# mLSTM outputs: the weights' upper part meets both parts of the values at once, and the sums lie in a pair of PSUM banks

## The chip, the cores and the metric

The kernel runs on one core of a Trainium2 chip. The metric is the device time of one execution in microseconds; shorter is better. The core's engines are TensorE (PE in the profile, with PEld for its weight loads), VectorE (DVE), ScalarE (ACT), GpSimd (POOL) and SyncE (SP, which issues most DMAs).

## The reference

One encoder layer over a prompt of 1024 tokens and a sample of 2048 tokens, each with 16 learned meta tokens in front. One input projection feeds two branches: neighbourhood attention and a bidirectional mLSTM. Both are gated, projected, merged and sent through an output projection. What matters here is the mLSTM output of one chunk (4 heads of 128; each direction has its own gates):

```python
S = jnp.einsum('bhnjd,bhnsd->bhnjs', q, k) * jnp.exp(logD - m_t[..., None])
e_inter = jnp.exp(inter - m_t)
num = jnp.einsum('bhnjs,bhnsv->bhnjv', S, v) + e_inter[..., None] * jnp.einsum('bhnvk,bhnjk->bhnjv', Cs, q)
den = jnp.sum(S, axis=-1) + e_inter * jnp.einsum('bhnk,bhnjk->bhnj', ns, q)
h = num / jnp.maximum(jnp.abs(den), jnp.exp(-m_t))[..., None]
```

Inputs and outputs are float32.

## The kernel before

**Products in two parts.** A float32 operand is split into an upper part (rounded to the type that PE multiplies in one pass, `F32R`) and a lower part (the rest). `mm3` makes one product out of three PE matmuls: upper by upper, upper by lower, lower by upper (lines 172, 173, 174). The same lines appear in the profile for every user of `mm3`, so tiles tell the users apart.

**Two streams of work in one order.** `dense` (input projection, merge, output projection) and `sparse` (mLSTM and attention of both sequences) are Python generators. `run` takes a step of the sparse one and then steps of the dense one in proportion to a rate, so PE's instructions are interleaved in an order fixed by hand. PE runs that order as it stands. The order on the other engines is planned by a scheduler that simulates the program; semaphores are put in by the framework. A tile with `bufs=n` rotates through n buffers, and the writer of a buffer waits for all readers of the tile that had it before.

**The mLSTM stage** (`ml`, once per sequence) first runs a gate chain (`ml_gates`, small matmuls, transposes and scans for both directions in turn), then for each of 4 heads `ml_states` (backward over blocks of 256 tokens, two chunks of 128 each) and `ml_outputs` (forward over blocks: 4 in the prompt, 8 in the sample, so 48 blocks and 96 chunks in all). In `ml_outputs`, for a block: `scores` multiplies keys by queries into bank `sc`; `weigh` applies decay and splits the result into `sh` and `sl`; `values` splits the values; `back(b, j)` for each of the two chunks j multiplies the query by the state (`pi`, 260 columns, in a `tr` bank), lets ACT scale that into `num` (line 1829), then multiplies the weights by the values, for each direction d with one `mm3` of 130 columns (128 values, a column of ones, one of zeros), and lets DVE add this to `num` (line 1834). `finish` divides. `back(p, 0)` and `back(p, 1)` of a block lie two steps of the generator apart, with dense work and `weigh`, `split`, `mask`, `chain` of the next block between.

**PSUM.** There are 8 banks of 512 floats per partition: tag `pj` has 3, `tr` 2, `sc` 1, `sm` 2. In the mLSTM stage `sm` serves the gate chain (one bank per small step), `pd` in `ml_states` (one bank per chunk), and `pa` in `back` (one bank per chunk, both directions side by side). In the attention stage `sm` serves scores and outputs.

```python
BANKS = dict(pj=3, tr=2, sc=1, sm=2)
```

Of the kernel before, what the change touches and what calls it, by code (L numbers as in the profile page):

```python
# [10 lines left out]
F32 = mybir.dt.float32  # L11
F32R = mybir.dt.float32r
I32 = mybir.dt.int32
AF = mybir.ActivationFunctionType
ALU = mybir.AluOpType
PSUM = bass.MemoryType.PSUM
DRAM = bass.MemoryType.DRAM

P = 128
# [18 lines left out]
CB = 2  # L38
# [88 lines left out]
class K:  # L127
# [36 lines left out]
            self.tc.keep_in_program_order(x)  # L164

    def psum(self, tag, shape):
        return self.pp.tile(shape, F32, name=tag, tag=tag, bufs=BANKS[tag])

    def mm3(self, out, ah, al, bh, bl, start=True, stop=True, **more):

# [6 lines left out]
    def setup(self, ctx):  # L177
        tc, nc, i = self.tc, self.nc, self.i
        self.cp = cp = ctx.enter_context(tc.tile_pool(name="cp", bufs=1))
        self.dp = dp = ctx.enter_context(tc.tile_pool(name="dp", bufs=1, space=DRAM))  # L180
        self.pp = ctx.enter_context(tc.tile_pool(name="pp", bufs=2, space=PSUM))
        self.ident = cp.tile([P, P], F32, name="ident")
        nc.sync.dma_start(self.ident, i["eye"])
        warm = cp.tile([P, 1], F32, name="warm")
        nc.gpsimd.memset(warm, 0.0)
        nc.scalar.activation(warm, warm, AF.Square)
        self.ones = cp.tile([P, P], F32, name="ones")
        nc.gpsimd.memset(self.ones, 1.0)
        p = self.psum("sm", [P, 4, P])
        o = self.ones.rearrange("p (a b) -> p a b", a=1).to_broadcast([P, 4, P])  # L190
        for _ in range(4):
            nc.tensor.matmul(p, self.ones, o, start=True, stop=True)
# [1235 lines left out]
    def ml_gates(self, s, keep, mp, res):  # L1428
# [33 lines left out]

        def one(d):
            l2 = lf[:, d].rearrange("p c h -> p (c h)")
            pb = self.psum("sm", [P, 512])
            nc.tensor.matmul(pb[:, :NR], self.tri[:, d, :], l2, start=True, stop=True)
            bT = t(f"g_b{d}", [P, NC_, 4])
            nc.vector.tensor_copy(bT.rearrange("p c h -> p (c h)"), pb[:, :NR])
            aT = kt(f"g_a{d}")
            nc.vector.tensor_tensor(aT, gv[:, d, 0], bT, op=ALU.subtract)  # L1470
            aTf = aT.rearrange("p c h -> p (c h)")
            yield
            pa = self.psum("sm", [P, 512])
            nc.tensor.transpose(pa[:NR, :P], aTf, self.ident)
            aR = t("g_aR", [NR, P], bufs=2)
            nc.scalar.activation(aR, pa[:NR, :P], AF.Copy)
            yield
            cm = t("g_cm", [NR, P], bufs=2)
            rv = (lambda x: x) if d == 0 else (lambda x: x[:, ::-1])
            nc.vector.tensor_tensor_scan(out=rv(cm), data0=rv(aR), data1=rv(aR), initial=-3.0e38, op0=ALU.max, op1=ALU.max)  # L1480
            end = P - 1 if d == 0 else 0
            pg = self.psum("sm", [P, 512])
            nc.tensor.matmul(pg[0:1, :NR], self.ones[:, 0:1], l2, start=True, stop=True)
            rg = t("g_rg", [1, NR], bufs=2)
            nc.scalar.activation(rg, pg[0:1, :NR], AF.Copy)
            yield
            px = self.psum("sm", [P, 512])
            nc.tensor.transpose(px[0:1, :NR], cm[:, end:end + 1], self.ident[:NR, :NR])
            ra = t("g_ra", [1, NR], bufs=2)
            nc.vector.tensor_tensor(ra, px[0:1, :NR], rg, op=ALU.add)  # L1490
            me = t("g_me", [1, NR], bufs=2)
            mpv = t("g_mp", [1, NR], bufs=2)
            nc.gpsimd.memset(mpv, 0.0)
            yield
            for h in range(4):
                w = slice(h, NR, 4)
                nc.vector.tensor_tensor_scan(out=rv(me[:, w]), data0=rv(rg[:, w]), data1=rv(ra[:, w]), initial=0.0,
                                             op0=ALU.add, op1=ALU.max)
            if d == 0:
                nc.vector.tensor_copy(mpv[:, 4:], me[:, :NR - 4])  # L1500
            else:
                nc.vector.tensor_copy(mpv[:, :NR - 4], me[:, 4:])
            yield
            pm = self.psum("sm", [P, 512])
            nc.tensor.transpose(pm[:NR, 0:1], mpv, self.ident[0:1, 0:1])
            mpc = t("g_mpc", [NR, 1], bufs=2)
            nc.vector.tensor_copy(mpc, pm[:NR, 0:1])
            uR = t("g_uR", [NR, P], bufs=2)
            nc.vector.tensor_scalar(uR, cm, mpc, -1.0, op0=ALU.max, op1=ALU.mult)
            nc.sync.dma_start(self.UD[s].rearrange("h c d t -> c h d t")[:, :, d, :], uR)  # L1510
            uend = t("g_ue", [NR, 1], bufs=2)
            nc.vector.tensor_copy(uend, uR[:, end:end + 1])
            nc.scalar.activation(cm, uR, AF.Exp, bias=mpc)
            nc.scalar.activation(aR, aR, AF.Exp, bias=uend)
            fs = t("g_fs", [NR, 1], bufs=2)
            nc.scalar.activation(fs, uend, AF.Exp, bias=mpc)
            yield
            pu = self.psum("sm", [P, 512])
            nc.tensor.transpose(pu[:, :NR], uR, self.ident[:NR, :NR])
            em = kt(f"g_em{d}")  # L1520
            nc.vector.tensor_tensor(em.rearrange("p c h -> p (c h)"), pu[:, :NR], bT.rearrange("p c h -> p (c h)"), op=ALU.subtract)
            nc.scalar.activation(em, em, AF.Exp)
            dg = t("g_dg", [NR, NR], bufs=2)
            nc.vector.tensor_scalar(dg, self.ident[:NR, :NR], fs, None, op0=ALU.mult)
            yield
            for name, x in (("e", cm), ("w", aR)):
                pe = self.psum("sm", [P, 512])
                nc.tensor.transpose(pe[:, :NR], x, self.ident[:NR, :NR])
                eT = kt(f"g_{name}T{d}")
                nc.vector.tensor_copy(eT.rearrange("p c h -> p (c h)"), pe[:, :NR])  # L1530
                out[d][name] = eT
                yield
            pf = self.psum("sm", [P, 512])
            nc.tensor.matmul(pf[:, :NR], self.ones[:NR, :], dg, start=True, stop=True)
            fsb = kt(f"g_fb{d}")
            nc.vector.tensor_copy(fsb.rearrange("p c h -> p (c h)"), pf[:, :NR])
            out[d].update(a=aT, em=em, f=fsb)
# [59 lines left out]
    def ml(self, s):  # L1597
# [3 lines left out]
        with tc.tile_pool(name=f"mg{s}", bufs=1, side="right", reuse_waits="tile") as keep:  # L1601
            with tc.tile_pool(name=f"mt{s}", bufs=1, side="right", reuse_waits="tile") as mp:
# [4 lines left out]
                    nc.sync.dma_start(self.trim[:, j], self.i["trimask"])  # L1607
                g = []
                yield from self.ml_gates(s, keep, mp, g)
            with tc.tile_pool(name=f"ml{s}", bufs=1, side="right", reuse_waits="tile") as mp:  # L1610
                self.vas = [mp.tile([P, CB, 130], F32, name=f"va{j}") for j in range(3)]
                for va in self.vas:
                    nc.gpsimd.memset(va[:, :, 128:129], 1.0)
# [17 lines left out]
                while norms:  # L1631
# [2 lines left out]
                    n += 1  # L1634
                    yield A_A
        self.done.add(("ml", s))

    def vload(self, mp, s, h, tok, np_, nch):
        nc = self.nc
# [6 lines left out]
    def ml_states(self, mp, s, h, g, NB, sts):  # L1646
# [34 lines left out]
        for i in range(N):  # L1681
# [13 lines left out]
            yield A_D  # L1695
            vwh, vwl = vws.pop(i)
            if not c0:
                pd = self.psum("sm", [P, 512])
                self.mm3(pd[:, :130], kth[:NM, 0, :], ktl[:NM, 0, :], vwh[:NM, 0, 0, :], vwl[:NM, 0, 0, :])
                nc.scalar.activation(sts[0][:, 0, 0:130], pd[:, :130], AF.Copy)  # L1700
                yield A_D
                continue
# [3 lines left out]
                nc.gpsimd.memset(sts[b][:, CB - 1, 130:260], 0.0)  # L1706
            if b:
                sts[b - 1] = mp.tile([P, CB, 260], F32, name="st", bufs=NB)
            for j in range(CB - 1, -1, -1):
                cc = b * CB + j  # L1710
                pd = self.psum("sm", [P, 512])
                self.mm3(pd[:, :260], kth[:, j, :], ktl[:, j, :],
                         vwh[:, j].rearrange("p d c -> p (d c)"), vwl[:, j].rearrange("p d c -> p (d c)"))
                if cc + 1 < NB * CB:
# [6 lines left out]
    def ml_outputs(self, mp, s, h, g, NB, sts, norms):  # L1721
# [44 lines left out]
        def values(b):  # L1766

            if b < NB:
                va = vas.pop(b)
                vh = mp.tile([P, CB, 130], F32R, name="vh", bufs=1)  # L1770
                vl = mp.tile([P, CB, 130], F32R, name="vl", bufs=1)
                nc.scalar.activation(f2(vh), f2(va), AF.Copy)
                nc.vector.tensor_tensor(f2(vl), f2(va), f2(vh).bitcast(F32), op=ALU.subtract)
                vs[b] = vh, vl

        def chain(b):

# [39 lines left out]

        def back(b, j):
            sh, sl = shs[b]
            (vh, vl), qx = vs[b], qks[b][:, 0]  # L1820
            cch, ccl = cs[b]
            cc = 1 + b * CB + j
            pi = self.psum("tr", [P, 512])
# [3 lines left out]
            num = nums[b]  # L1827
            for d in range(2):
                nc.scalar.activation(num[:, j, d], pi[:, 130 * d:130 * d + 130], AF.Copy, scale=g[d]["e"][:, cc, h:h + 1])
            pa = self.psum("sm", [P, 512])  # L1830
            for d in range(2):
                self.mm3(pa[:, 130 * d:130 * d + 130], sh[:, j, d, :], sl[:, j, d, :], vh[:, j, :], vl[:, j, :])
            nj = num[:, j].rearrange("p d c -> p (d c)")
            nc.vector.tensor_tensor(nj, pa[:, :260], nj, op=ALU.add)

        def finish(b):
            num = nums.pop(b)
# [429 lines left out]
```

## Time and profile before

| what | value |
|---|---|
| median of 3 runs (lowest, highest) | 2720.48 us (2719.08, 2722.17) |
| profiled execution, its time | 2718.74 us |
| its span in the profile | 2717.0 us |
| PE busy | 2686.7 us, 99% |
| DVE busy | 1766.1 us, 65% |
| ACT busy | 1520.2 us, 56% |
| granted PE clock, mean | 0.998 |

A row of a group reads: line, engine, operation, output<-inputs by tile names, partitions x elements, count, then time. A row of the timeline reads: start in us from the span's start, duration in us, engine, line, operation, tiles, shapes, count, and in brackets the idle time of the engine before it with what ended that. Durations on PE overlap, since matmuls are pipelined; the distance from one start to the next tells what one costs. A row of a stretch of time gives, after the stretch, the busy time of PE, PEld, DVE, ACT and POOL (with counts), the granted clock, the DMA share and the bandwidth. A row of waits reads: who waited on whose tile, then microseconds in total, times, longest.

### The profile page before, as it was taken

Reading aid. Unit: us, or ns where it says so; the run is one execution under the profiler, and the core shown is the slowest. Engines: PE = TensorE matmul, PEld = TensorE weight load, DVE = VectorE, ACT = ScalarE, POOL = GpSimd, SP = SyncE. Lnnn points to the kernel's source line nnn. Section 1 sums busy time; section 2 is a strip of 40 time slices with the busy share of each in tenths; the row PEclk is TensorE's granted clock in tenths of the full one; section 3 lists DMA queues with packets and bytes.
Section 4 is the critical chain, followed back from the end, with each engine's and each line's share of the span. In section 5 each row is a group of like instructions: output and inputs, shape, how many; then the busy total and the mean of one; then the engine's idle time right before and its main releaser. Section 6 shows DMA issues by size and latency. Waiting matters only on the chain.

```text
span 2717.0 us, 47583 instructions
## 1 busy us (share of the span) xinstructions
PE 2686.7 (99%) x16696; PEld 2394.5 (88%) x16696; DVE 1766.1 (65%) x4376; ACT 1520.2 (56%) x3375; POOL 126.0 (5%) x294
## 2 busy tenths in 40 slices
PE   9999999999999999999999999999999999999998
PEld 7999988879998889998878888888879898989988
DVE  5557765535777747775424857574658879687864
ACT  5233354435555656666535757564648686767641
POOL 0005000005000013000000000000000000000000
PEclk9999999999999999999999999999999999999999
DMA  9984454369865797757486666786599999898955
GB/s 369 340 283 143 138 187 158 102 239 343 265 222 174 264 325 227 229 175 234 144 294 191 222 202 209 262 278 201 163 299 332 313 298 295 245 317 244 324 208 220
DMA packets 351507, 657.53 MB, mean 242 GB/s; under 512 B 53444, under 2 KB 158868, under 8 KB 351268
## 3 DMA queue, kind: packets, MB, share of 16 engines
q1 hardware_dynamic: 344004, 645.46, 71.7%
q0 software_dynamic: 7264, 9.04, 1.2%
q8 instruction: 131, 2.15, 0.3%
q14 instruction: 108, 0.88, 0.1%
HBM read 438.64 MB, written 215.66 MB: 241 GB/s over the span
## 4 chain that ended last, share of the span: by engine, by line
PE 88%; DMA 7%; DVE 2%; ACT 2%; issue 1%; SPq 1%; POOL 0%; DVEq 0%; ACTq 0%; POOLq 0%
PE pj L172 14%; PE pj L173 14%; PE pj L174 14%; PE pj L644 5%; PE pj L645 5%; PE pj L646 5%; PE sm L1407 3%; PE pj L2042 2%; PE pj L2044 2%; PE pj L2043 2%; PE tr L1393 2%; PE sm L174 2%; PE sm L173 2%; PE sm L172 2%; DMA wraw<-wu 1%; DMA wlo<-wl 1%
## 5 line engine op out<-in xcount | busy, mean ns | idle before, releaser
L172 PE MATMUL pj<-xh,whi 128*128 128x512 f32 (+1 forms) x1480 | 580.2, 392 | 4.6 <-ACT st L569 3.6
L173 PE MATMUL pj<-xl,whi 128*128 128x512 f32 (+1 forms) x1480 | 565.8, 382 | 0.2 <-DVE xl L345 0.2
L174 PE MATMUL pj<-xh,wlo 128*128 128x512 f32 (+1 forms) x1480 | 565.1, 382 | 0.3 <-DVE wlo L272 0.3
L644 PE MATMUL pj<-whi,xh 128*128 128x256 f32 (+1 forms) x1152 | 330.9, 287 | 0.0
L174 PEld LDWEIGHTS pj<-xh,wlo 128*128 128x128 f32 x1480 | 278.2, 188 | 58.2 <-DVE wlo L272 0.6
L172 PEld LDWEIGHTS pj<-xh,whi 128*128 128x128 f32 x1480 | 278.5, 188 | 54.1 <-ACT st L569 4.4
L645 PE MATMUL pj<-wlo,xh 128*128 128x256 f32 (+1 forms) x1152 | 325.0, 282 | 0.6 <-DMA wlo<-wl 0.6
L646 PE MATMUL pj<-whi,xl 128*128 128x256 f32 (+1 forms) x1152 | 324.8, 282 | 0.0
L173 PEld LDWEIGHTS pj<-xl,whi 128*128 128x128 f32 x1480 | 278.8, 188 | 46.2 <-issue 0.7
L2042 PE MATMUL pj<-whi,mh 128*128 128x256 f32 x768 | 220.3, 287 | 0.0
L645 PEld LDWEIGHTS pj<-wlo,xh 128*128 128x128 f32 x1152 | 217.1, 188 | 0.9 <-DMA wlo<-wl 0.8
L644 PEld LDWEIGHTS pj<-whi,xh 128*128 128x128 f32 x1152 | 217.3, 189 | 0.4
L646 PEld LDWEIGHTS pj<-whi,xl 128*128 128x128 f32 x1152 | 217.0, 188 | 0.0
L2043 PE MATMUL pj<-wlo,mh 128*128 128x256 f32 x768 | 217.0, 283 | 0.0
L2044 PE MATMUL pj<-whi,mlo 128*128 128x256 f32 x768 | 216.9, 282 | 0.0
L1396 DVE TENSOR_TENSOR pts<-tr,pts 96x384 fp32r<-96x384 f32 (+2 forms) x192 | 118.5, 617 | 64.7 <-ACT pts L1395 63.8
L172 PE MATMUL pj<-yh,whi 128*128 128x512 f32 x384 | 154.2, 401 | 1.8 <-DVE tg L2009 1.1
L173 PE MATMUL pj<-yl,whi 128*128 128x512 f32 x384 | 151.0, 393 | 0.2 <-DVE yl L1420 0.2
L174 PE MATMUL pj<-yh,wlo 128*128 128x512 f32 x384 | 151.0, 393 | 0.0
L2043 PEld LDWEIGHTS pj<-wlo,mh 128*128 128x128 f32 x768 | 146.1, 190 | 1.0
L2042 PEld LDWEIGHTS pj<-whi,mh 128*128 128x128 f32 x768 | 146.0, 190 | 1.0
L2044 PEld LDWEIGHTS pj<-whi,mlo 128*128 128x128 f32 x768 | 145.9, 190 | 0.0
(459 smaller groups left out, 6171.7 us busy)
## 6 DMA issues: line engine op xcount, KB each, us to landing
whi<-wh SPq DMA_DIRECT2D x140, 512.0 KB
wlo<-wl SPq DMA_DIRECT2D x140, 512.0 KB
wraw<-wu SPq DMA_DIRECT2D x64, 512.0 KB
wh<-whi SPq DMA_DIRECT2D x64, 512.0 KB
wl<-wlo SPq DMA_DIRECT2D x64, 512.0 KB
gt<-st SPq DMA_DIRECT2D x96, 256.0 KB
tg<-gt SPq DMA_DIRECT2D x96, 256.0 KB
xt<-xt SPq DMA_DIRECT2D x32, 512.0 KB
```

Of the source, the lines that this page charges most:

```text
L172: mm(out, ah, bh, start=start, stop=False, **more)
L173: mm(out, ah, bl, start=False, stop=False, **more)
L174: mm(out, al, bh, start=False, stop=stop, **more)
L644: nc.tensor.matmul(o, xh, wh, start=k == 0, stop=False)
L645: nc.tensor.matmul(o, xh, wl, start=False, stop=False)
L646: nc.tensor.matmul(o, xl, wh, start=False, stop=k == KT - 1)
L1393: nc.tensor.transpose(pt[:ks, ch, :], pr_[:, ch * ks:(ch + 1) * ks], self.ident)
L1396: nc.vector.tensor_tensor(pts[:ks, :nb, 1, :], pt[:ks, :nb], pts[:ks, :nb, 0, :].bitcast(F32), op=ALU.subtract)
L1407: nc.tensor.matmul(av[:, cb % 2], vt[:ks, kc // 8 + ch].rearrange("p a b -> p (a b)"), pts[:ks, ch].rearrange("p a b -> p (a b)"), start=c ...
L2042: nc.tensor.matmul(o, mh[:, f, xs], q, start=fresh and f == 0, stop=False, skip_group_check=True)
L2043: nc.tensor.matmul(o, mh[:, f, xs], w[1][:, k, :], start=False, stop=False, skip_group_check=True)
L2044: nc.tensor.matmul(o, ml[:, f, xs], q, start=False, stop=f == KT - 1, skip_group_check=True)
```

## The change

- `values` writes both parts into one tile `v` of shape [P, 2, 2, 130], part by part next to each other within a chunk.
- `back` takes a pair of banks for a chunk, one bank for a direction. For each direction the lower part of the weights meets the upper part of the values (130 columns), then the upper part of the weights meets both parts in one matmul of 258 columns: columns 0 to 129 accumulate, columns 130 to 257 are a sum of their own. DVE adds the first 130 columns of both banks to `num`, and then the other 128 columns of both.
- The two banks of `sm` get a pool of their own that is closed in the mLSTM's states and outputs. There a pool `pl` holds one tile of two banks: `pa` of `back`, and in `ml_states` one tile for both chunks of a block.
- The gate chain takes its banks from `tr` instead of `sm`.
- In `setup` the tags `pj`, `tr` and `sc` are allocated once at the start.

```diff
     def psum(self, tag, shape):
-        return self.pp.tile(shape, F32, name=tag, tag=tag, bufs=BANKS[tag])
+        return (self.pm if tag == "sm" else self.pp).tile(shape, F32, name=tag, tag=tag, bufs=BANKS[tag])
+
+    def small(self, on):
+
+        if on:
+            self.sms = ExitStack()
+            self.pm = self.sms.enter_context(self.tc.tile_pool(name=f"pm{len(self.done)}", bufs=2, space=PSUM))
+        else:
+            self.sms.close()
...
         self.pp = ctx.enter_context(tc.tile_pool(name="pp", bufs=2, space=PSUM))
+        for tag in ("pj", "tr", "sc"):
+            self.psum(tag, [P, 512])
+        self.small(True)
+        ctx.callback(lambda: self.small(False))
...
         def one(d):
             l2 = lf[:, d].rearrange("p c h -> p (c h)")
-            pb = self.psum("sm", [P, 512])
+            pb = self.psum("tr", [P, 512])
...
                 yield from self.ml_gates(s, keep, mp, g)
-            with tc.tile_pool(name=f"ml{s}", bufs=1, side="right", reuse_waits="tile") as mp:
+            self.small(False)
+            with tc.tile_pool(name=f"ml{s}", bufs=1, side="right", reuse_waits="tile") as mp, \
+                 tc.tile_pool(name=f"pl{s}", bufs=1, space=PSUM) as self.pl:
...
         self.done.add(("ml", s))
+        self.small(True)
...
             if not c0:
-                pd = self.psum("sm", [P, 512])
+                pd = self.pl.tile([P, 2, 512], F32, name="pa")[:, 0]
...
+            pds = self.pl.tile([P, CB, 512], F32, name="pa")
             for j in range(CB - 1, -1, -1):
                 cc = b * CB + j
-                pd = self.psum("sm", [P, 512])
+                pd = pds[:, j]
...
-                vh = mp.tile([P, CB, 130], F32R, name="vh", bufs=1)
-                vl = mp.tile([P, CB, 130], F32R, name="vl", bufs=1)
-                nc.scalar.activation(f2(vh), f2(va), AF.Copy)
-                nc.vector.tensor_tensor(f2(vl), f2(va), f2(vh).bitcast(F32), op=ALU.subtract)
-                vs[b] = vh, vl
+                v = vs[b] = mp.tile([P, CB, 2, 130], F32R, name="vh", bufs=1)
+                nc.scalar.activation(v[:, :, 0], va, AF.Copy)
+                nc.vector.tensor_tensor(v[:, :, 1], va, v[:, :, 0].bitcast(F32), op=ALU.subtract)
...
-            pa = self.psum("sm", [P, 512])
+            pa = self.pl.tile([P, 2, 512], F32, name="pa")
             for d in range(2):
-                self.mm3(pa[:, 130 * d:130 * d + 130], sh[:, j, d, :], sl[:, j, d, :], vh[:, j, :], vl[:, j, :])
-            nj = num[:, j].rearrange("p d c -> p (d c)")
-            nc.vector.tensor_tensor(nj, pa[:, :260], nj, op=ALU.add)
+                nc.tensor.matmul(pa[:, d, 0:130], sl[:, j, d, :], v[:, j, 0], start=True, stop=False, skip_group_check=True)
+                nc.tensor.matmul(pa[:, d, 0:258], sh[:, j, d, :], v[:, j].rearrange("p a c -> p (a c)")[:, 0:258], start=False, stop=True, skip_group_check=True)
+            nj = num[:, j]
+            nc.vector.tensor_tensor(nj, pa[:, :, 0:130], nj, op=ALU.add)
+            nc.vector.tensor_tensor(nj[:, :, 0:P], pa[:, :, 130:258], nj[:, :, 0:P], op=ALU.add)
```

The seven other places of the gate chain change from `sm` to `tr` in the same way.

More of the change, by code (lines that the diff above doesn't have):

```diff
@@ L1472, in one @@
             yield
-            pa = self.psum("sm", [P, 512])
+            pa = self.psum("tr", [P, 512])
             nc.tensor.transpose(pa[:NR, :P], aTf, self.ident)
@@ L1481, in one @@
             end = P - 1 if d == 0 else 0
-            pg = self.psum("sm", [P, 512])
+            pg = self.psum("tr", [P, 512])
             nc.tensor.matmul(pg[0:1, :NR], self.ones[:, 0:1], l2, start=True, stop=True)
@@ L1486, in one @@
             yield
-            px = self.psum("sm", [P, 512])
+            px = self.psum("tr", [P, 512])
             nc.tensor.transpose(px[0:1, :NR], cm[:, end:end + 1], self.ident[:NR, :NR])
@@ L1503, in one @@
             yield
-            pm = self.psum("sm", [P, 512])
+            pm = self.psum("tr", [P, 512])
             nc.tensor.transpose(pm[:NR, 0:1], mpv, self.ident[0:1, 0:1])
@@ L1517, in one @@
             yield
-            pu = self.psum("sm", [P, 512])
+            pu = self.psum("tr", [P, 512])
             nc.tensor.transpose(pu[:, :NR], uR, self.ident[:NR, :NR])
@@ L1526, in one @@
             for name, x in (("e", cm), ("w", aR)):
-                pe = self.psum("sm", [P, 512])
+                pe = self.psum("tr", [P, 512])
                 nc.tensor.transpose(pe[:, :NR], x, self.ident[:NR, :NR])
@@ L1532, in one @@
                 yield
-            pf = self.psum("sm", [P, 512])
+            pf = self.psum("tr", [P, 512])
             nc.tensor.matmul(pf[:, :NR], self.ones[:NR, :], dg, start=True, stop=True)
@@ L1819, in back @@
             sh, sl = shs[b]
-            (vh, vl), qx = vs[b], qks[b][:, 0]
+            v, qx = vs[b], qks[b][:, 0]
             cch, ccl = cs[b]
@@ L1829, in back @@
                 nc.scalar.activation(num[:, j, d], pi[:, 130 * d:130 * d + 130], AF.Copy, scale=g[d]["e"][:, cc, h:h + 1])
-            pa = self.psum("sm", [P, 512])
+            pa = self.pl.tile([P, 2, 512], F32, name="pa")
             for d in range(2):
-                self.mm3(pa[:, 130 * d:130 * d + 130], sh[:, j, d, :], sl[:, j, d, :], vh[:, j, :], vl[:, j, :])
-            nj = num[:, j].rearrange("p d c -> p (d c)")
-            nc.vector.tensor_tensor(nj, pa[:, :260], nj, op=ALU.add)
+                nc.tensor.matmul(pa[:, d, 0:130], sl[:, j, d, :], v[:, j, 0], start=True, stop=False, skip_group_check=True)
[3 more added lines that the diff above has]
+            nc.vector.tensor_tensor(nj[:, :, 0:P], pa[:, :, 130:258], nj[:, :, 0:P], op=ALU.add)
         def finish(b):
```

## Prediction

> **What bounds the kernel now.** I read the page first: the span and the busy line.
>
> ```profile
> span 2717.0 us, 47583 instructions
> ...
> PE 2686.7 (99%) x16696; PEld 2394.5 (88%) x16696; DVE 1766.1 (65%) x4376; ACT 1520.2 (56%) x3375; POOL 126.0 (5%) x294
> ```
>
> PE is idle for 30 us of 2717 and runs one order written out by hand, so the time is the sum of what its instructions take plus what it waits. Anything that shortens PE work shortens the span, as long as no other engine makes PE wait. VectorE (DVE) has room on average, but the average hides the mLSTM stages, so next I looked up the changed instructions by tile (count, shortest/median/longest in ns, first and last start, shapes).
>
> ```profile
> L1834 DVE TENSOR_TENSOR num<-sm,num x96: 393/428/430, 665.8 to 1977.8; 128x260 f32<-128x260 f32 x96
> ```
>
> The add of `back` stands here 96 times (two chunks in each of 48 blocks); ahead of each add PE runs six 130-column products, three for each direction. The durations of PE overlap, so I price PE by the distance between starts, from the timeline. The first and the last of the 96 groups of six:
>
> ```profile
> 663.96 0.23 PE L172 MATMUL sm<-vh,sh 128*128 128x130 f32 x1
> ...
> 664.47 0.28 PE L174 MATMUL sm<-vh,sl 128*128 128x130 f32 x1
> 664.58 0.33 PE L644 MATMUL pj<-whi,xh 128*128 128x256 f32 x1
> 664.75 0.28 PE L645 MATMUL pj<-wlo,xh 128*128 128x256 f32 x1
> 664.87 0.28 PE L646 MATMUL pj<-whi,xl 128*128 128x256 f32 x1
> ```
>
> ```profile
> 1976.90 0.23 PE L172 MATMUL sm<-vh,sh 128*128 128x130 f32 x1
> ...
> 1977.53 0.44 PE L172 MATMUL pj<-xh,whi 128*128 128x512 f32 x1
> ```
>
> The group takes 0.62 us (663.96 to 664.58), and 0.63 at the end. The product behind it takes 0.17 (to 664.75) where the next one of its size takes 0.12 (to 664.87): 0.05 of the group's cost shows there. So six products of 130 columns cost 0.67, or 0.11 each, almost what 256 columns cost. Below some width a product here costs its weight load, not its columns.
>
> **The change, part by part.**
>
> *Products of `back`.* Six products of 130 columns with six weight loads become four: per direction the weights' lower part meets 130 columns and the upper part meets 258. The kernel already has this mix: `scores` runs 256, 128, 256, 128 columns with four loads.
>
> ```profile
> 654.21 0.28 PE L1799 MATMUL sc<-qkx 128*128 128x256 f32 x1
> 654.32 0.22 PE L1801 MATMUL sc<-qkx 128*128 128x128 f32 x1
> 654.38 0.34 PE L1799 MATMUL sc<-qkx 128*128 128x256 f32 x1
> 654.56 0.23 PE L1801 MATMUL sc<-qkx 128*128 128x128 f32 x1
> 654.62 0.33 PE L644 MATMUL pj<-whi,xh 128*128 128x256 f32 x1
> ```
>
> It takes 0.41 us (654.21 to 654.62), and with the same 0.05 behind it 0.46, that is 0.12 for the wide and 0.11 for the narrow one. The changed group ends on a wide product, so it shows 0.46 itself and nothing behind. Saving: 0.67 − 0.46 = 0.21; with the medians of the starts over all groups it is 0.670 − 0.463 = 0.207, and 96 × 0.207 = 19.9 us of PE. The ends for this term: 2 × 0.11 = 0.22 per group if two narrow products vanish whole (21 us), and 0.67 − 4 × 0.12 = 0.19 if all four cost as much as a wide one (18 us). I take 19.9, since `scores` is nearly the same instructions.
>
> *The second add.* The sum now lies in two parts of a pair of banks, so a DVE add of 2×130 is followed by one of 2×128. The nearest row is an add of 256 elements out of a bank:
>
> ```profile
> L1804 DVE TENSOR_TENSOR ss<-ss,sc x48: 390/421/424, 655.6 to 1963.9; 128x256 f32<-128x256 f32 x48
> ```
>
> That is 0.42 us long; but DVE's instructions overlap, and the two adds of the row at 921.95 further down lie 0.33 to 0.34 apart (0.75 for both, less 0.42 for one). 96 × 0.34 = 33 us of DVE, all in the mLSTM stages. DVE by stage:
>
> ```profile
> 905.00:943.00 38.00, 38.00 (x205) 32.34 (x204) 35.73 (x97) 27.67 (x65) 2.92 (x12) 1.00 0.62 195
> 1903.00:1980.00 77.00, 77.00 (x422) 66.01 (x422) 50.83 (x178) 46.78 (x124) 2.38 (x8) 1.00 0.53 159
> ```
>
> The third busy figure is DVE: 50.8 of 77 us in the last head of the long sequence, which takes 16 × 0.34 = 5.4 more without trouble, but 35.7 of 38 in the last head of the short one, where eight groups bring 2.7 more and PE gets 1.7 faster: 38.4 into 36.3. There DVE becomes the limit, by 2 us.
>
> *One pair of banks where there were two single ones.* This is the new wait. Today the two groups of a block use different banks. After, the second group's first product must wait until both adds of the first group have read the pair. Behind it in PE's queue stands everything, the dense projection included; no DMA or SP or POOL instruction is added or moved. An add that comes at once is no problem:
>
> ```profile
> 665.84 0.43 DVE L1834 TENSOR_TENSOR num<-sm,num 128x260 f32<-128x260 f32 x1 [0.41 <-ACT num L1829]
> ...
> 667.88 0.23 PE L172 MATMUL sm<-vh,sh 128*128 128x130 f32 x1
> ```
>
> The add ends at 666.27, 1.61 us before the second group begins. I call this the margin. But the adds stand in DVE's and ACT's queues and are often late, which costs nothing today. I went through all 48 pairs; the first, the worst and the last of the bad ones:
>
> ```profile
> 677.71 0.22 PE L172 MATMUL sm<-vh,sh 128*128 128x130 f32 x1
> ...
> 677.90 0.42 DVE L1834 TENSOR_TENSOR num<-sm,num 128x260 f32<-128x260 f32 x1
> ```
>
> ```profile
> 915.08 0.23 PE L172 MATMUL sm<-vh,sh 128*128 128x130 f32 x1
> ...
> 918.90 0.22 PE L172 MATMUL sm<-vh,sh 128*128 128x130 f32 x1
> ...
> 921.95 0.75 DVE L1834 TENSOR_TENSOR num<-sm,num 128x260 f32<-128x260 f32 x2
> ```
>
> ```profile
> 1945.86 0.41 DVE L1834 TENSOR_TENSOR num<-sm,num 128x260 f32<-128x260 f32 x1
> ...
> 1946.62 0.23 PE L172 MATMUL sm<-vh,sh 128*128 128x130 f32 x1
> ```
>
> Margins: −0.61, −3.47 (first of the two adds in that row) and +0.36. The new need is 0.65: 0.34 for the second add, 0.21 because PE comes earlier, and an estimate of 0.1 for the signal, by the group of 1976.90, whose add starts 0.11 behind the last product's end. Of the 48 margins 13 lie under it: six below zero, three of those in the head of 915, and seven from 0.26 to 0.54. They sum to −5.3, so the shortfall is 13 × 0.65 + 5.3 = 13.8 us if every pair pays alone. It won't: once PE has waited 4.1 us at 918.9, DVE has caught up, and the next two pairs of that head, 2.3 and 1.8 short, mostly don't pay. I take 9.7; the ends are 0 (the order of DVE and ACT is made anew and puts the adds first) and, with adds 0.75 later everywhere from the added DVE work, 26 over the same 48 margins. The margin from the second group to the next block's first is at least 2 us in all cases.
>
> *States.* The two products of a block now share one tile, so the next block waits for all its drains, not for one bank's. The tightest case:
>
> ```profile
> 1590.26 0.34 DVE L1717 SCALAR_TENSOR_TENSOR st<-st,g_fb,sm 128x130 f32<-128x130 f32 x1
> ...
> 1590.69 0.39 PE L172 MATMUL sm<-vwh,kt 128*128 128x260 f32 x1
> ```
>
> The last drain ends 0.09 ahead of it, and everywhere else 0.8 or more. I take 0; what hides it is the dense work between two blocks, and if that cover goes it is 0.3 us in one place. A gain has no room: PE waits for nothing there now.
>
> *Gate chain on the transposes' banks, and the pools.* Same instructions, again two banks; while a chain runs nothing else uses those banks, and the mLSTM begins only after it. The longest wait of PE inside a chain:
>
> ```profile
> PE sm L1519 <- DVE g_uR L1509: 0.5, 1, 0.5
> ```
>
> I take 0, and ±1 us (twice that row) as its ends, since each step of a chain passes the two banks on as it did. Closing and reopening the pool waits for readers that ended many microseconds before. The split of the values writes the same 260 elements per instruction: 0.
>
> *Sum.* −19.9 + 9.7 = −10.2; with some room for a better order of the adds I say −11. The profiled execution is 2718.74 with a span of 2717.0; it becomes 2707.7. The median of the runs is 2720.48, 1.7 above that execution, so the forecast for the median is **2709.5 us**.
>
> **The rivals.**
>
> *The whole saving arrives.* No add is late in the new order: −19.9, 2700.5. For it: PE is in one line, and the order of the other engines is planned again with the new wait in it. Against: the head of 915 lacks DVE time whatever the order.
>
> *The pair eats it all.* Stalls between 14 and 25 us: 2715 to 2726. The Trainium skill, "Perfetto Trace Analysis", section "Optimizing Tensor Performance", says that independent matmul groups should rotate through different banks, so that the evacuation of one overlaps the next group's products; by that rule this change takes the overlap away. Today's traces bear it out for 13 pairs of 48; in the other 35 the 3.2 us of other PE work between the groups (915.08 to 918.90, less 0.62) covers the evacuation.
>
> *Slower: every add comes later.* The mechanism is the release of the pair by DVE in the mLSTM heads. It cancels the gain at 19.9/48 = 0.41 us of stall per pair and makes the kernel measurably slower at 0.53; with the margins as they are that takes adds 0.75 us later throughout (26 us, 2726.6). At 1.5 us later it is 48 us and 2748. For it: 33 us more DVE work; against it: in the head from 1903 a third of DVE's time is free (50.8 of 77).
>
> *The products save nothing.* If columns alone set the pace, 780 columns become 776 and only the stalls remain: 2730. By the narrow product's 0.06 (654.32 to 654.38) six would be 0.36, and four 2 × 0.06 + 2 × 0.12 = 0.36. But the group of six does take 0.62, so I give this little. The Trainium skill, "TensorE: Matmul & The Clock Gate", section "Back-to-back issue gap", has this as the isolated gap, N/2.4 + 2.5 ns; an estimate by it is 0.34 us before and 0.33 after, where the trace has 0.62 before.
>
> **How the numbers follow.** Forecast with stalls of 4 to 14 us: 0.55 (2704.5 to 2714.5). Whole saving, stalls under 4: 0.20. All eaten: 0.16. Slower by later adds: 0.07; columns: 0.02. Measurement tells 0.2%, 5.4 us, from no change. Faster: 0.55 + 0.20 = 0.75; within: 0.16; slower: 0.09. The range runs from 2699 (the whole saving, a little beyond) to 2721 (half of "eaten"); it leaves out the largest gains by a better order and the slower cases.
>
> **What would show it.** Right: groups of four in 0.46 us; PE work down by about 20 us; waits of PE for the add at its first product of the second group, a dozen, longest near 4 us, mostly in the head around 915; a second add of 0.42. Wrong: groups of four that take 0.6; no wait at that product (then −20); waits at most pairs, or new waits for weights and DVE in the stages behind, where the planned order of the other engines has come out differently.

## The result, and the profile after

The changed kernel takes 2782.89 us (median of 4 runs, 2777.10 to 2787.36) against 2721.32 us before (four runs, one more than in the table above): ratio 1.0234, 95% interval 1.0218 to 1.0250, 62 us slower. The prediction said 2709.5 and put 0.09 on slower. The profiled execution took 2777.1 us; its page begins:

```profile
span 2775.3 us, 47329 instructions
...
PE 2690.5 (97%) x16504; PEld 2383.7 (86%) x16504; DVE 1800.6 (65%) x4472; ACT 1523.2 (55%) x3375; POOL 126.1 (5%) x294
```

PE issues 192 products fewer, as planned, and yet its idle time is now 85 us where it was 30. (Line 172 of before is 180 here, 1834 has become 1849 and 1850.) PE's waits, in total, times, longest:

```profile
PE pa L180 <- DVE st L1733: 44.9, 48, 2.5
PE pa L1846 <- DVE num L1850: 8.6, 6, 5.5
...
PE pa L1846 <- DVE mv L1921: 2.8, 3, 1.2
...
PE pa L1846 <- DVE mv L1923: 1.4, 2, 0.9
...
PE pa L1846 <- DVE ss L447: 0.6, 1, 0.6
```

The last four rows (12 waits, 13.4 us) are the wait that the prediction was about. Where a row names `mv` or `ss`, the add had ended just before: the wait that ended at 1574.78 came 0.14 us behind the end of its add. The first row is not in the prediction: L180 on `pa` is the first product in `ml_states`, and 48 is once per block, each time at the block's second chunk. Its timeline, after, with both engines that drain the bank:

```profile
1472.69 0.28 PE L180 MATMUL pa<-vwh,kt 128*128 128x260 f32 x1
1472.69 0.19 PEld L181 LDWEIGHTS pa<-vwl,kt 128*128 128x128 f32 x1
1472.81 0.28 PE L181 MATMUL pa<-vwl,kt 128*128 128x260 f32 x1
...
1472.93 0.28 PE L182 MATMUL pa<-vwh,kt 128*128 128x260 f32 x1
...
1474.36 0.27 ACT L1731 ACTIVATE st<-pa 128x130 f32<-128x130 f32 x1
...
1474.67 0.35 DVE L1733 SCALAR_TENSOR_TENSOR st<-st,g_fb,pa 128x130 f32<-128x130 f32 x1 [0.32 <-ACT st L1731]
...
1475.07 0.19 PEld L180 LDWEIGHTS pa<-vwh,kt 128*128 128x128 f32 x1 [2.07 <-DVE st L1733]
1475.07 0.39 PE L180 MATMUL pa<-vwh,kt 128*128 128x260 f32 x1 [1.86 <-DVE st L1733]
...
1475.30 0.28 PE L181 MATMUL pa<-vwl,kt 128*128 128x260 f32 x1
...
1475.54 0.39 PE L180 MATMUL pj<-xh,whi 128*128 128x512 f32 x1
```

The same place before, PE alone:

```profile
1426.42 0.28 PE L174 MATMUL sm<-vwh,kt 128*128 128x260 f32 x1
1426.55 0.29 PE L172 MATMUL sm<-vwh,kt 128*128 128x260 f32 x1
1426.67 0.28 PE L173 MATMUL sm<-vwl,kt 128*128 128x260 f32 x1
...
1426.91 0.39 PE L172 MATMUL pj<-xh,whi 128*128 128x512 f32 x1
```

Before, the second chunk's products followed the first chunk's after 0.13 us (1426.42 to 1426.55; the median of the 48 places is 0.12). After, they start 2.14 us behind (1472.93 to 1475.07): first ACT and then DVE drain the first chunk, one behind the other, and only then does PE go on, although the second chunk writes the other bank. The row of waits understates this, since the durations of PE are modelled to overlap: 2.14 − 0.12 is 2.02 us lost where the row counts 1.86. With 0.16 more at each of 48 places the loss is 44.9 + 7.7 = 52.6 us; from start to start, summed over all 48, it is 58.8 after less 6.2 before, the same 52.6.

A second cost, the slow start, follows each wait, and no row of waits shows it. The first product behind the wait holds PE for 0.23 us (1475.07 to 1475.30), where without a wait it is 0.12 (1426.55 to 1426.67). Its weight load begins only when the product does (1475.07), while the load of the product at 1472.81 began a product earlier (1472.69). Over the 48 places the second chunk's three products take 22.5 us after and 17.3 before, 5.2 more.

The products themselves do what was forecast. The first group of four, after:

```profile
668.22 0.23 PE L1846 MATMUL pa<-vh,sl 128*128 128x130 f32 x1
668.28 0.33 PE L1847 MATMUL pa<-vh,sh 128*128 128x258 f32 x1
668.45 0.22 PE L1846 MATMUL pa<-vh,sl 128*128 128x130 f32 x1
668.51 0.33 PE L1847 MATMUL pa<-vh,sh 128*128 128x258 f32 x1
668.68 0.28 PE L656 MATMUL pj<-whi,xh 128*128 128x256 f32 x1
668.80 0.28 PE L657 MATMUL pj<-wlo,xh 128*128 128x256 f32 x1
```

It takes 0.46 us (668.22 to 668.68) and the product behind it its usual 0.12.

The longest wait at the pair is where the prediction looked for it, in the last head of the prompt, and it shows a cost on top of the wait. First PE around it, then rows of four stretches of time:

```profile
935.63 0.28 PE L182 MATMUL tr<-cch,qkx 128*128 128x260 f32 x1
941.38 0.45 PE L1846 MATMUL pa<-vh,sl 128*128 128x130 f32 x1 [5.46 <-DVE num L1850]
941.62 0.52 PE L1847 MATMUL pa<-vh,sh 128*128 128x258 f32 x1
941.94 0.31 PE L1846 MATMUL pa<-vh,sl 128*128 128x130 f32 x1
942.05 0.52 PE L1847 MATMUL pa<-vh,sh 128*128 128x258 f32 x1
```

```profile
938.00:944.00 6.00, 2.62 (x8) 2.34 (x9) 5.53 (x13) 4.11 (x11) 1.19 (x3) 0.50 0.70 209
945.00:952.00 7.00, 7.00 (x39) 5.94 (x37) 6.93 (x24) 3.27 (x8) 0.00 (x0) 1.00 0.82 269
1754.00:1757.00 3.00, 3.00 (x10) 2.31 (x10) 1.52 (x5) 1.45 (x5) 0.00 (x0) 0.50 0.99 315
802.00:806.00 4.00, 3.92 (x33) 3.92 (x34) 1.98 (x8) 2.03 (x7) 0.00 (x0) 1.00 0.63 203
```

After PE had idled, the granted clock (third figure from the end) was 0.50 from 938 to 944, and the second 130-column product, which takes 0.06 in the group of 668.22, took 0.11 (941.94 to 942.05). The first one took 0.24, clock and late weight load together; at full clock the first one behind a wait takes 0.14 (1574.78 to 1574.92). The same half clock stands at 1754, behind a shorter wait of the states; but a wait of the same length, which ended at 802.08, has full clock behind it:

```profile
802.08 0.39 PE L180 MATMUL pa<-vwh,kt 128*128 128x260 f32 x1 [2.08 <-DVE st L1733]
...
1753.37 0.39 PE L180 MATMUL pa<-vwh,kt 128*128 128x260 f32 x1 [2.07 <-DVE st L1733]
```

The mean granted clock is 0.996 after and 0.998 before; 0.002 of 2775 is 5.5 us, an estimate, since both means are rounded.

The Trainium skill, "TensorE: Matmul & The Clock Gate", section "Why this matters for your kernels", warns of PE gaps over about 3 us, behind which the clock falls back to half; the first case agrees with it (5.46 us), the second has half clock behind a shorter gap (2.07 us).

The sum by these rows: −19.9 for the products, +52.6 for the waits of the states, +15.3 for the pair (13.4 in four rows and 0.16 at each of 12 places), +5.5 for the clock make +53.5, and the spans differ by 58.3. The slow starts fill the gap: 5.2 in the states and about 1.0 at the pair (0.14 for 0.06 at 12 places) bring the sum to 59.7.

### The profile page after: what moved, and what is told of

Same layout as the page of the kernel before. It is cut to its first block, busy times and chain, and to the rows that moved or that the text cites. A ratio compares the mean times of both kernels' runs of the same rounds, so it can differ in the third digit from the quotient of the medians.

```text
span 2775.3 us, 47329 instructions
## 1 busy us (share of the span) xinstructions
PE 2690.5 (97%) x16504; PEld 2383.7 (86%) x16504; DVE 1800.6 (65%) x4472; ACT 1523.2 (55%) x3375; POOL 126.1 (5%) x294
## 4 chain that ended last, share of the span: by engine, by line
PE 81%; DMA 8%; DVE 6%; ACT 3%; issue 2%; SPq 1%; POOL 0%; DVEq 0%; ACTq 0%; POOLq 0%
PE pj L180 13%; PE pj L181 13%; PE pj L182 13%; PE pj L656 5%; PE pj L658 4%; PE pj L657 4%; PE sm L1419 3%; PE pj L2058 3%; PE pj L2060 3%; PE pj L2059 3%; PE tr L1405 2%; DMA wraw<-wu 1%; PE pa L1847 1%; PE pa L180 1%; PE sm L182 1%
## 5 line engine op out<-in xcount | busy, mean ns | idle before, releaser
L180 PE MATMUL pj<-xh,whi 128*128 128x512 f32 (+1 forms) x1480 | 579.9, 392 | 2.6 <-ACT st L581 2.3
L180 PEld LDWEIGHTS pj<-xh,whi 128*128 128x128 f32 x1480 | 280.2, 189 | 52.4 <-ACT st L581 3.0
L180 PE MATMUL pj<-yh,whi 128*128 128x512 f32 x384 | 154.1, 401 | 0.7 <-ACT yh L1431 0.7
```

The source lines that it names most:

```text
L180: mm(out, ah, bh, start=start, stop=False, **more)
```

## The experiments

Theory A: the tile that both chunks of a states block now share makes the second chunk's products wait for the first chunk's drains, and this is the loss. Rival B: the pair in the outputs and the 33 us of added DVE work are the cause, and the states only show a lateness. Each time stands beside runs of the kernel before on the same chip (medians 2717.2 to 2718.3); in brackets stands the 95% interval of the ratio. The two-tile version, the three built on it and the version with the shared tile alone also open and close the pools once per head, where the changed kernel does so once per sequence.

**Two tiles for the states** (the two-tile version). Only the outputs keep the pair.

```diff
-            pds = self.pl.tile([P, CB, 512], F32, name="pa")
...
-                pd = pds[:, j]
+                pd = self.psum("sm", [P, 512])
```

> The changed kernel, but the states keep their two chunks in two tiles of one bank each; only the outputs use the pair. Theory A (the shared states tile makes the second chunk's products wait for the first chunk's drains; 45 us of PE waits in the trace after, and some of the throttled clock behind them): those waits vanish, PE waits on pa in the outputs stay near 15 us, and the time falls to 2715 to 2730. Rival B (the outputs' pair and the 33 us of added DVE work are the cause, and the states only show a lateness that would show elsewhere): it stays above 2765, with waits on other tiles in place of the states'.

Measured 2716.66 us against 2717.50: 0.9996 (0.9987 to 1.0005). The 48 waits are gone, B has fallen, and the rest of the change gains nothing. Its waits on the pair:

```profile
PE pa L1845 <- DVE num L1849: 9.7, 7, 5.4
...
PE pa L1845 <- DVE mv L1920: 1.8, 2, 1.2
...
PE pa L1845 <- DVE mv L1922: 1.1, 2, 0.9
```

**The shared tile alone, in the kernel before.** The outputs keep six products and single banks.

```diff
+            pds = self.pl.tile([P, CB, 512], F32, name="pa")
...
-                pd = self.psum("sm", [P, 512])
+                pd = pds[:, j]
```

> The kernel before, with one part of the change alone: the two chunks of a states block share one tile of two banks; the outputs run as before with six products and single banks. Theory A: 48 PE waits of about 1 us on pa, each for DVE's drain of the first chunk, and the time rises by 45 to 60 us to 2766 to 2781. Rival B: no more than 5 us above the kernel before.

Measured 2780.69 us: 1.0234 (1.0217 to 1.0250), 63 us slower: within the range of the time, 3 us over that of the rise. This one edit alone costs as much as the whole change, whose other parts come out even in the two-tile version. Its row:

```profile
PE pa L180 <- DVE st L1733: 41.5, 48, 2.4
```

With 0.16 more per place that is 49 us. The slow starts add 5.6 (22.9 for the second chunk's products where 17.3 stood), and the granted clock fell to 0.996 here too (5.5 by the same estimate). These make 60; the two spans differ by 60.4, the medians by 63.

**The same shared tile, drains behind both chunks' products.** The changed kernel with one loop cut in two:

```diff
             for j in range(CB - 1, -1, -1):
-                cc = b * CB + j
-                pd = pds[:, j]
-                self.mm3(pd[:, :260], kth[:, j, :], ktl[:, j, :],
+                self.mm3(pds[:, j, :260], kth[:, j, :], ktl[:, j, :],
                          vwh[:, j].rearrange("p d c -> p (d c)"), vwl[:, j].rearrange("p d c -> p (d c)"))
+            for j in range(CB - 1, -1, -1):
+                cc = b * CB + j
+                pd = pds[:, j]
```

> The changed kernel with the same shared tile and the same banks in the states, but both chunks' products are issued ahead of all drains, so that no drain of the tile stands between them. Theory A (the wait follows from the order in which a tile is written, read and written again, not from the banks): the 48 waits vanish as with two tiles, 2715 to 2730. Rival C (the pair of banks itself must be free of readers, whatever the order): the waits move to the next block's first product and the time stays above 2750.

Measured 2723.04 us: 1.0018 (1.0009 to 1.0028). The tile and its two banks are those of the changed kernel, and 60 us are gone; C has fallen. So no bank needs the wait: it comes from a tile that is written, read and written again in program order. That the framework orders such a tile as a whole is what these runs together say; no run looks into the framework. What is left, at the next block:

```profile
PE pa L180 <- DVE st L1734: 1.9, 3, 0.9
```

That is the wait which the prediction did look for in the states, and took for 0; in the changed kernel itself it was 0, since all 48 waits stand at the second chunk. The remaining question is why this and the two-tile version gain nothing.

**The wide products in a single bank.** The kernel before, per direction 130 and then 256 columns, so that both directions fit one bank and two banks rotate; two adds. The lower part of the last two value columns is left out.

```diff
-                self.mm3(pa[:, 130 * d:130 * d + 130], sh[:, j, d, :], sl[:, j, d, :], vh[:, j, :], vl[:, j, :])
+                mm(pa[:, 256 * d:256 * d + 130], sl[:, j, d, :], v[:, j, 0], start=True, stop=False, skip_group_check=True)
+                mm(pa[:, 256 * d:256 * d + 256], sh[:, j, d, :], v[:, j].rearrange("p a c -> p (a c)")[:, 0:256], start=False, stop=True, skip_group_check=True)
...
+            nc.vector.tensor_tensor(nj[:, :, 0:126], pv[:, :, 130:256], nj[:, :, 0:126], op=ALU.add)
```

> The kernel before with the wide product alone: per direction 130 columns and then 256 (130 of the upper part, 126 of the lower), so that both directions fit into one bank and two banks rotate as before; two adds. It leaves out the lower part of the last two value columns. If the price of the products in the prediction holds (0.207 us per group, 96 groups) and the second add is hidden where nothing waits for the bank: 2721 - 20 = 2701, within 2698 to 2706, and groups of four in 0.41 to 0.46 us. If the added DVE work is itself a cost (rival B): 2715 or more.

Measured 2700.46 us: 0.9944 (0.9927 to 0.9961), 17 us faster by the medians and 11 to 20 by the interval, so the 19.9 of the prediction lie at its upper end. The first group of four takes 0.46 (665.61 to 666.07). The two-tile version is 16.2 us slower than this one, and its pair accounts for about that: 11 waits of 12.6 us in the rows above, 0.16 more at each for the overlap and about 0.08 for the slow start make 15.2.

**The same without the second add.**

```diff
-            nc.vector.tensor_tensor(nj[:, :, 0:126], pv[:, :, 130:256], nj[:, :, 0:126], op=ALU.add)
```

> The single-bank version with wide products (2700.5 us) without its second add; it leaves out the products of the weights' upper part with the values' lower part. Theory D: the added DVE work costs nothing where no PE instruction waits for it soon: 2697 to 2703. Rival F: 33 us of DVE are worth 5 us or more: under 2695.

Measured 2701.02 us: 0.9934 (0.9922 to 0.9946). The second add costs nothing where no PE instruction waits for it soon.

**The pair alone, with six products and one add** (on the two-tile version):

```diff
-                nc.tensor.matmul(pa[:, d, 0:130], sl[:, j, d, :], v[:, j, 0], start=True, stop=False, skip_group_check=True)
-                nc.tensor.matmul(pa[:, d, 0:258], sh[:, j, d, :], v[:, j].rearrange("p a c -> p (a c)")[:, 0:258], start=False, stop=True, skip_group_check=True)
+                self.mm3(pa[:, d, 0:130], sh[:, j, d, :], sl[:, j, d, :], v[:, j, 0], v[:, j, 1])
...
-            nc.vector.tensor_tensor(nj[:, :, 0:P], pa[:, :, 130:258], nj[:, :, 0:P], op=ALU.add)
```

> The version with two states tiles, but the outputs make their six products of 130 columns and one add of 2x130 as before; only the pair of banks with its one buffer is left of the change in the outputs. Theory D: the pair costs by itself; by the 48 margins of the kernel before with a need of 0.1 us the shortfall is 8.8 us, about 5 after catching up: 2721 to 2727, with PE waits on pa of 4 to 9 us. Rival F (the waits come from the 33 us of the second add, not from the pair): no waits on pa over 2 us, 2715 to 2720.

Measured 2729.28 us: 1.0044 (1.0032 to 1.0057), 12 us slower, more than D's range.

```profile
PE pa L180 <- DVE num L1847: 6.2, 6, 3.4
...
PE pa L180 <- DVE nwt L156: 0.6, 1, 0.6
```

The pair costs by itself; F has fallen as the whole story. In the two-tile version the second add and the faster PE together go with almost twice the waits, 12.6 us for 6.8. The 6.8 with what goes along with each wait explain some 8 of the 12 us; the rest stays open.

**The adds kept in program order** (on the two-tile version; the same for ACT's scaling):

```diff
-            nc.vector.tensor_tensor(nj, pa[:, :, 0:130], nj, op=ALU.add)
-            nc.vector.tensor_tensor(nj[:, :, 0:P], pa[:, :, 130:258], nj[:, :, 0:P], op=ALU.add)
+            self.behind(nc.vector.tensor_tensor(nj, pa[:, :, 0:130], nj, op=ALU.add))
+            self.behind(nc.vector.tensor_tensor(nj[:, :, 0:P], pa[:, :, 130:258], nj[:, :, 0:P], op=ALU.add))
```

> The version with two states tiles (2716.7 us), where ACT's scaling into num and both adds are in addition kept in the program's order on their engines, so that the planner can't put later work ahead of them. Theory D (what is left of the loss, 16 us against the single-bank version, is PE waiting at the pair for adds that stand late in DVE's and ACT's queues): PE's waits on pa fall from 12.6 us to under 4 and the time to 2700 to 2709. Rival E (DVE and ACT lack the time in those heads whatever the order): waits on pa stay over 8 us and the time within 5 us of 2716.7, or grows as other work now stands behind the adds.

Measured 2808.24 us: 1.0330 (1.0315 to 1.0344), the opposite of D; a growth is what E allows for at its end. Waits on the pair, and ACT near the end of the longest:

```profile
PE pa L1845 <- DVE num L1849: 78.3, 17, 17.6
```

```profile
930.19 0.63 ACT L1579 ACTIVATE cpl<-cpl,cw 128x400 f32<-128x400 f32 x1 [6.18 <-DMA cpl<-mk]
930.73 0.61 ACT L1842 ACTIVATE num<-tr,g_eT 128x130 f32<-128x130 f32 x2
```

Kept in order, the scaling stands behind a convolution step that waits for its DMA (6.18 of the 17.6 us here; what makes up the rest is open), and the adds, hence PE, behind both. The planner's freedom, which I took for the cause of the late adds, here also moved them ahead of work that isn't ready.

**The first chunk's products one step earlier** (on the two-tile version):

```diff
             if b < NB:
                 scores(b)
-            yield A_A
             if p >= 0:
                 back(p, 0)
+            yield A_A
```

> The version with two states tiles (2716.7 us), where the first chunk's products of a block are issued one generator step earlier, right behind the scores, so that three steps of dense work instead of two lie between the two users of the pair, and two instead of three ahead of the next block. Theory D (PE waits at the pair only because the adds have 3.8 us there and some need more; by the margins of the kernel before, with 1.9 us more only the pair at 915 is short): PE waits on pa fall under 5 us, and the time to 2702 to 2711. Rival E (DVE and ACT are short of time, so the waits move to the other gap of the block): waits on pa stay over 8 us and the time over 2713.

Measured 2716.93 us: 0.9991 (0.9981 to 1.0001), no gain. The numbers are those of E, but not its mechanism: all eight waits on the pair still stand at a block's second group, whose gap was widened, and none moved to the other gap.

```profile
PE pa L1845 <- DVE num L1849: 5.9, 5, 2.3
...
PE pa L1845 <- DVE mv L1922: 3.6, 3, 2.4
...
PE pa L1846 <- DVE vh L1787: 2.3, 4, 1.2
```

The longest wait at the pair falls from 5.4 to 2.4, but 9.5 us stay there and 2.3 appear on the values, which now have a step less of lead. A wider gap alone doesn't remove the waits.

**One direction wide.** The kernel before, whole computation, 388 columns in one bank, two banks in turn:

```diff
+            self.mm3(pa[:, 0:130], sh[:, j, 0, :], sl[:, j, 0, :], v[:, j, 0], v[:, j, 1])
+            mm(pa[:, 130:260], sl[:, j, 1, :], v[:, j, 0], start=True, stop=False, skip_group_check=True)
+            mm(pa[:, 130:388], sh[:, j, 1, :], v[:, j].rearrange("p a c -> p (a c)")[:, 0:258], start=False, stop=True, skip_group_check=True)
...
+            nc.vector.tensor_tensor(num[:, j, 1, 0:P], pa[:, 260:388], num[:, j, 1, 0:P], op=ALU.add)
```

> The kernel before, whole computation, with the wide product for one direction alone: 130, 130, 130 columns for the first and 130, 258 for the second, 388 columns in one bank, two banks in turn; the second add has 128 elements. By the prices of the prediction one narrow product less per chunk, 96 x 0.104 = 10 us: 2717.5 - 10 = 2707.5, within 2704 to 2711, and no PE waits on this tile over 2 us. Rival F: half of the added DVE work shows: 2713 or more.

Measured 2712.63 us: 0.9988 (0.9979 to 0.9997). It beats both kernels and leaves nothing out, but by 0.8 to 5.7 us of 2717 where 10 were forecast. The median lies between the forecast range and that of F, so it decides neither. The first group of five and the product behind it:

```profile
663.63 0.22 PE L172 MATMUL sm<-vh,sh 128*128 128x130 f32 x1
...
664.03 0.34 PE L1832 MATMUL sm<-vh,sh 128*128 128x258 f32 x1
664.20 0.29 PE L644 MATMUL pj<-whi,xh 128*128 128x256 f32 x1
664.33 0.28 PE L645 MATMUL pj<-wlo,xh 128*128 128x256 f32 x1
```

With the product behind it the group takes 0.70 us (663.63 to 664.33), where six and the product behind them take 0.79 (663.96 to 664.75 in the kernel before), so about 0.1 per chunk is there. Where the rest of the 10 us went is not settled.

## Why the prediction was wrong, point by point

- **The products: right.** 19.9 us were forecast, by the row of `scores`. The group of four takes 0.46 as forecast, and the single-bank version is 17 us faster (11 to 20). PE's busy time, which was to fall by 20 us, is no sign of it here: it went from 2686.7 to 2690.5 in the changed kernel, where products behind a wait and at half clock count longer, and to 2671.6 in the two-tile version. With one direction wide, at most 5.7 of the 10 us show, and why stays open.
- **The step that failed: "States. ... I take 0".** It asked what the next block waits for, and that term was right (0; 1.9 us where the drains come last). ("PE waits for nothing there now" holds for the banks; for the keys it waited 2.0 us in five places, and 1.5 after.) It didn't ask what the second chunk of the same block waits for. The program writes chunk 1, drains it, then writes chunk 0; with both in one tile the second write stands behind the drains. The trace of before showed what was at stake: PE's next three products follow the first three at once (1426.42 to 1426.55), with both drains still to come. 48 such places, with 52.6 us of waits, 5.2 of slow starts and some throttled clock, are as much as the whole loss, as the experiment with this edit alone shows (63 us).
- **The rivals: none held this.** The slower rival put the waits in the outputs. The rule of different banks, on which the rival with the pair eating it all drew, was weighed for the outputs only. It names the right kind of harm, but not this case: in the states the banks did differ, and the overlap was lost because the tile was one.
- **The pair in the outputs: mechanism right, term mis-sized.** 9.7 us were forecast. The rows of waits after give 13.4, and the pair is worth 16.2 between two versions that otherwise differ by two value columns' lower part, the gate chain's banks and the pools. The longest wait was 5.46 where 4.1 was forecast, in the head named. That there are a dozen, as forecast, is partly luck: most were expected in that head, and one of the twelve stands there.
- **The second add: right that it is hidden by itself** (2701.0 without it, 2700.5 with it); wrong that it only counts by DVE's load, since behind the pair it goes with nearly doubled waits (6.8 and 12.6 us, the faster PE included).
- **The clock and the slow start** were not in the sum. A wait of PE can cost again afterwards: by estimate 5.5 us at half clock and 6.2 at the first products here.
- **Gate chain and pools at 0: nothing speaks against it, but no run changes them alone.** The longest wait inside a chain is 0.5 us again, and the two-tile version, which holds both, stands at 0.9996 with about 15 us of the pair against the products' 17 to 20.

```profile
PE tr L1531 <- DVE g_uR L1521: 0.5, 1, 0.5
```

## What to carry to other kernels

When two buffers become one tile with two halves, list every write, read and write of that tile in program order, within one iteration too: here the second write waited for the first half's readers although the halves are different banks. Either keep separate tiles or issue all writes ahead of all reads. Before an in-order engine is given a single buffer, measure how late its readers are today: a reader's delay that costs nothing with two buffers becomes that engine's idle time.

## What was not expected of the hardware

Half clock followed some waits well under the long one: the stretch from 1754 has 0.50 behind a wait of 2.07 us in the states. The wait of 2.08 us that ended at 802.08 has 1.00 behind it, so length alone doesn't tell them apart, and what does is open. The kernel with the longest waits (the order kept) ran at a mean clock of 0.981. With that and the slow start of 0.23 for 0.12 us, an estimate of a wait's cost on PE from its length alone is too low here.
